# Moving the low-part subtractions of the even output projection's weights from VectorE to GpSimd

## Chip, cores and metric

One core of one Trainium2 chip runs the whole program in one launch. The metric is the device time in microseconds (us) of that core. All times below come from the runs of the kernel before, or from the trace of one profiled execution of it.

## What is computed

The reference is a two-layer decoder trunk over 256 tokens of width 1024, in float32. Cut to what matters:

```
for i in range(2):
    h = h + 0.5 * swiglu(rms_norm(h, ffa_norm[i]), ffa_w_gate_up[i], ffa_w_down[i])
    hn = rms_norm(h, mix_norm[i])
    h = h + (even_mixer(hn, ...) if i % 2 == 0 else odd_mixer(hn, ...))
    h = h + 0.5 * swiglu(rms_norm(h, ffb_norm[i]), ffb_w_gate_up[i], ffb_w_down[i])
    gate = sigmoid(rms_norm(h, ple_norm[i]) @ ple_w_gate[i])
    h = h + gate * (p[i] @ ple_w_proj[i])
return rms_norm(h, final_norm)
# even_mixer: a_q,a_k,a_v,c_q,c_kv,k_rope = split(hn @ w_in)
#   out_a = sliding-window attention with sinks (8 heads)
#   out_b = attention with low-rank q (w_uq) and kv (w_ukv), rotary part on q and k (8 heads)
#   return concatenate([out_a, out_b]) @ w_out          (1024 x 1024)
```

## The kernel before, in words

The 256 tokens are two blocks of 128 rows, t = 0 and t = 1. Each block is a Python generator (`stream`, `even`, `odd`, `ffn`, `ple`), and a loop at the end of `trunk` lets the two take turns, so that both blocks use a weight piece while it is in SBUF.

Every weight matrix is multiplied at higher precision than one pass gives: a piece is loaded as float32 into a raw tile `wr`, ScalarE (ACT) casts it to the high part `wh` (float32r), and VectorE (DVE) subtracts it from the raw piece to give the low part `wl` (`split_steps`). A product is then three matmuls: high times high, high times low, low times high. For weights without a norm gain the cast is line 240 and the subtraction line 241, both in steps of 128 x 512; with a gain they are lines 247 and 248. A list `order` holds all pieces in the order of their use; a piece is loaded four places ahead (`PREFETCH_DMA`, SP's queue, lines 221 to 226) and split one place ahead (`PREFETCH_SPLIT`). There are four raw tiles (`RAW_BUFS`) and four pairs of `wh` and `wl` (`SPLIT_BUFS`). So the load of piece i+4 waits until cast and subtraction of piece i are done, and the split of piece i+4 waits until TensorE (PE) has used piece i for both blocks.

The even output projection is `add_square("ev_out", ...)`: four pieces of 256 rows by 1024 columns, keys ("ev_out", 0) to ("ev_out", 3), no gain, each split in four steps. In `order` they stand behind the even input projection (five pieces), `uq` and `ukv`, and ahead of the second FFN's weights. Their splits therefore run while the even mixer does its attention:

- `even` makes q, k and v of both attentions: kvq scaled by ACT, the rotary part of q by DVE (lines 675, 677, 679), the rotary part of k copied into `k_f` by GpSimd (POOL) (line 753), v by DVE (line 760), then transposes by PE (line 685).
- `attend` (lines 576 to 615), for each group of heads: scores by PE (576), mask and row maximum by DVE (582), exp by ACT (588), the sink's share (594 to 596), reciprocal (598), scaling of the probabilities by DVE (600, P_sb times rinv, both in SBUF), transposes by PE (605), copy by ACT (607), product with v by PE (615).
- `mm_square` (365, 366, 369) is the output projection; line 366 is the matmul that reads `wl`.

The order of the instructions on each engine is not the program's: but for those that are pinned, a planner at build time places them by priority, by dependence and by its own estimate of each instruction's cost. Each engine then works through its list strictly in order, and waits at the head of the list for semaphores of the others. GpSimd's list in this stretch holds memsets, the two copies into `k_f` and DMAs of small tensors.

Of the kernel before, what the change touches and what calls it, by code (L numbers as in the profile page):

```python
# [10 lines left out]
F32 = mybir.dt.float32  # L11
# [30 lines left out]
def trunk(ctx, tc, a, out):  # L42
    nc = tc.nc
    pe, act, dve, pool = nc.tensor, nc.scalar, nc.vector, nc.gpsimd
# [17 lines left out]
    def pin(ins):  # L62

        return tc.keep_in_program_order(ins) if starting[0] else ins
# [76 lines left out]
    order = []  # L141
# [27 lines left out]
    for l in range(2):  # L169
        add_ffn("ffa", l)  # L170
        if l == 0:
            w = a["ev_w_in"][0]
            g = gcols["mix", 0]
            for i, k0 in enumerate((0, 3, 6)):
                kt = min(3, KD - k0)
# [50 lines left out]
            nc.sync.dma_start(r[:, :kt * n].rearrange("p (k f) -> p k f", k=kt), src)  # L226

    def split_steps(i):
        _, _, kt, n, g = order[i]
        r = raw_tiles.pop(i)  # L230
        wh = wsp.tile([P, 2048], F32R, name="wh", tag="wh")
        wl = wsp.tile([P, 2048], F32R, name="wl", tag="wl")
        tot = kt * n
        step_ = 512 if g is None else n // -(-n // 512)
        c0 = 0
        while c0 < tot:
            c1 = min(c0 + step_, tot)
            yield
            if g is None:
                pin(act.copy(wh[:, c0:c1], r[:, c0:c1]))  # L240
                pin(dve.tensor_tensor(wl[:, c0:c1], r[:, c0:c1], wh[:, c0:c1].bitcast(F32),  # L241
                                      op=ALU.subtract))
            else:
                k = c0 // n
                c1 = min(c1, (k + 1) * n)
                gc = gcol[:, g + k:g + k + 1]
                pin(act.mul(wh[:, c0:c1], r[:, c0:c1], gc))  # L247
                pin(dve.scalar_tensor_tensor(wl[:, c0:c1], r[:, c0:c1], gc,  # L248
                                             wh[:, c0:c1].bitcast(F32),
                                             op0=ALU.mult, op1=ALU.subtract))  # L250
            c0 = c1
        split_tiles[i] = (wh[:, :tot].rearrange("p (k f) -> p k f", k=kt),
                          wl[:, :tot].rearrange("p (k f) -> p k f", k=kt))
# [4 lines left out]
    def emit_split(i, steps=99):  # L258
        if i not in splits:
            splits[i] = split_steps(i)  # L260
            next(splits[i])
        for _ in range(steps):
            if next(splits[i], END) is END:
                break
# [807 lines left out]
    def at(st):  # L1072

        return index.get(st[1] if st and st[0] == "both" else st)
# [18 lines left out]
    while step != [END, END]:  # L1093
# [8 lines left out]
        else:  # L1102
            i = at(step[0]) if at(step[0]) is not None else place[0]
# [41 lines left out]
```

## Time and profile before

| | |
|---|---|
| median of 3 runs | 1045.86 us (1045.84, 1045.86, 1048.33) |
| the profiled execution | 1046.14 us, its span 1044.4 us |
| PE busy | 1026.4 us (98%) |
| DVE busy | 759.9 us (73%) |
| ACT busy | 651.1 us (62%) |
| POOL busy | 21.9 us (2%) |
| DMA, mean | 173 GB/s |

The span is what the trace covers; 1.7 us lie around it. An engine's busy time is the sum over the whole span; a change in one stretch has to be read from that stretch. In the views, "idle before" is the time for which an engine stood still ahead of an instruction, with what ended it. The chain of waits follows the work that ended last backwards through what released each step. Line numbers are those of the kernel.

### The profile page before, as it was taken

The numbers are of one execution on the slowest core, as the hardware profiler recorded it, in microseconds if no ns is written. First come the engines' busy times: TensorE is split into PE (matmuls) and PEld (weight loads), VectorE is DVE, ScalarE is ACT, GpSimd is POOL, SyncE is SP. The second block draws the span as 40 slices with busy tenths as digits, with TensorE's granted clock in tenths as the row PEclk, the third lists the DMA queues.
The fourth block names the chain that finished last, engine by engine and source line by source line (L and its number), as shares of the span: only waits on it lengthen the run. The fifth ranks groups of instructions, "written<-read, shape, count | busy, mean of one in ns | idle before, by whom it ended". The sixth has DMA issues, their size and how long they took to land.

```text
span 1044.4 us, 15663 instructions
## 1 busy us (share of the span) xinstructions
PE 1026.4 (98%) x5675; PEld 886.2 (85%) x5675; DVE 759.9 (73%) x1736; ACT 651.1 (62%) x1369; POOL 21.9 (2%) x50
## 2 busy tenths in 40 slices
PE   8999999998999999999999999999999999999996
PEld 6888888977888888888888888889998888888885
DVE  6876776888587676768868676688874868676685
ACT  6756566767576666566865656564655865656563
POOL 1000000010100000000100000001000000000000
PEclk9999999999999999999999999999999999999999
DMA  9855646453063646546565564644343465564611
GB/s 306 251 199 178 225 143 222 131 172 122 21 221 130 235 163 200 205 158 193 163 219 172 192 202 161 242 138 148 122 143 121 157 206 172 191 207 156 243 41 40
DMA packets 122189, 180.43 MB, mean 173 GB/s; under 512 B 6192, under 2 KB 96624, under 8 KB 122112
## 3 DMA queue, kind: packets, MB, share of 16 engines
q1 hardware_dynamic: 121200, 177.93, 50.8%
q0 software_dynamic: 624, 1.12, 0.3%
q8 instruction: 44, 0.72, 0.3%
q10 hardware_dynamic: 288, 0.39, 0.1%
q14 instruction: 33, 0.27, 0.1%
HBM read 178.34 MB, written 1.08 MB: 172 GB/s over the span
## 4 chain that ended last, share of the span: by engine, by line
PE 93%; DVE 3%; ACT 2%; issue 1%; DMA 1%; SPq 0%; ACTq 0%
PE tr L482 14%; PE gu L482 14%; PE acc L366 10%; PE acc L365 10%; PE acc L369 10%; PE tr L485 7%; PE gu L485 7%; PE gu L352 3%; PE gu L358 3%; PE gu L357 3%; PE acc L615 2%; PE tr L333 1%; PE tr L576 1%; PE gu L857 1%; PE gu L859 1%
## 5 line engine op out<-in xcount | busy, mean ns | idle before, releaser
L248 DVE SCALAR_TENSOR_TENSOR wl<-wr,gcol,wh 128x512 fp32r<-128x512 f32 (+2 forms) x462 | 327.4, 737 | 110.0 <-PE tr L485 88.1
L247 ACT ACTIVATE wh<-wr,gcol 128x512 fp32r<-128x512 f32 (+2 forms) x462 | 296.8, 707 | 131.6 <-PE acc L369 111.6
L482 PE MATMUL gu<-xT,wh 128*128 128x512 f32 x640 | 250.2, 391 | 0.0
L482 PE MATMUL tr<-xT,wh 128*128 128x512 f32 x640 | 249.6, 390 | 0.0
L241 DVE TENSOR_TENSOR wl<-wr,wh 128x512 fp32r<-128x512 f32 x216 | 136.2, 682 | 10.1 <-PE tr L485 5.8
L482 PEld LDWEIGHTS gu<-xT,wh 128*128 128x128 f32 x640 | 120.3, 188 | 23.6 <-ACT wh L247 0.2
L482 PEld LDWEIGHTS tr<-xT,wh 128*128 128x128 f32 x640 | 120.4, 188 | 23.6
L366 PE MATMUL acc<-wl,hT 128*128 128x512 f32 x352 | 137.6, 391 | 0.0
L365 PE MATMUL acc<-wh,hT 128*128 128x512 f32 x352 | 137.5, 391 | 0.0
L240 ACT CAST wh<-wr 128x512 fp32r<-128x512 f32 x216 | 125.3, 619 | 16.5 <-PE acc L369 11.0
L369 PE MATMUL acc<-wh,hT 128*128 128x512 f32 x352 | 109.2, 391 | 0.0
L485 PEld LDWEIGHTS gu<-xT,wl 128*128 128x128 f32 x640 | 86.8, 190 | 5.7
L485 PE MATMUL gu<-xT,wl 128*128 128x256 f32 x640 | 90.1, 283 | 0.0
L485 PE MATMUL tr<-xT,wl 128*128 128x256 f32 x640 | 89.8, 283 | 0.0
L485 PEld LDWEIGHTS tr<-xT,wl 128*128 128x128 f32 x640 | 82.5, 192 | 0.0
L369 PEld LDWEIGHTS acc<-wh,hT 128*128 128x128 f32 x352 | 66.1, 188 | 13.9
L365 PEld LDWEIGHTS acc<-wh,hT 128*128 128x128 f32 x352 | 66.3, 188 | 12.6 <-ACT hT L319 0.4
L366 PEld LDWEIGHTS acc<-wl,hT 128*128 128x128 f32 x352 | 66.3, 188 | 12.4
L490 ACT COPY sg<-gu 128x256 f32<-128x256 f32 x80 | 29.3, 366 | 74.2 <-PE gu L485 74.2
L491 DVE TENSOR_TENSOR sg<-sg,gu 128x256 f32<-128x256 f32 x80 | 33.4, 417 | 53.8 <-ACT sg L490 53.8
L319 ACT CAST hT<-sg 128x256 fp32r<-128x256 f32 x80 | 32.5, 406 | 43.0 <-DVE sg L513 43.0
L352 PE MATMUL gu<-wh,xT 128*128 128x512 f32 (+1 forms) x128 | 50.1, 392 | 0.0
(259 smaller groups left out, 1445.1 us busy)
## 6 DMA issues: line engine op xcount, KB each, us to landing
wr<-in_ffb_w_gate_up_dram SPq DMA_DIRECT2D x88, 512.0 KB, 5.3
wr<-in_ffa_w_gate_up_dram SPq DMA_DIRECT2D x84, 512.0 KB, 5.6
wr<-in_ffa_w_down_dram SPq DMA_DIRECT2D x22, 1024.0 KB, 5.0
wr<-in_ffb_w_down_dram SPq DMA_DIRECT2D x22, 1024.0 KB, 5.0
wr<-in_od_w_in_dram SPq DMA_DIRECT2D x12, 1024.0 KB, 5.1
wr<-in_ple_w_gate_dram SPq DMA_DIRECT2D x8, 1024.0 KB, 5.1
wr<-in_ev_w_out_dram SPq DMA_DIRECT2D x4, 1024.0 KB, 4.9
wr<-in_od_w_out_dram SPq DMA_DIRECT2D x4, 1024.0 KB, 5.4
```

The source lines that it names most:

```text
L240: pin(act.copy(wh[:, c0:c1], r[:, c0:c1]))
L241: pin(dve.tensor_tensor(wl[:, c0:c1], r[:, c0:c1], wh[:, c0:c1].bitcast(F32), op=ALU.subtract))
L247: pin(act.mul(wh[:, c0:c1], r[:, c0:c1], gc))
L248: pin(dve.scalar_tensor_tensor(wl[:, c0:c1], r[:, c0:c1], gc, wh[:, c0:c1].bitcast(F32), op0=ALU.mult, op1=ALU.subtract))
L319: pin(act.copy(dst_h, src))
L352: pe.matmul(dst, xh, wh, start=first, stop=False)
L365: pe.matmul(accs[n], xh, wh[:, kk, c], start=first, stop=False)
L366: pe.matmul(accs[n], xh, wl[:, kk, c], start=False, stop=False)
L369: pe.matmul(accs[n], xl, wh[:, kk, c], start=False, stop=last)
L482: pe.matmul(bv[s], w, xT[:, :, :, k, :], start=(k == 0), stop=False, skip_group_check=True)
L485: pe.matmul(bv[s][:, :, 0], w, xT[:, :, 0, k, :], start=False, stop=(k == KD - 1), skip_group_check=True)
L491: dve.tensor_tensor(o, o, bv[s][:, :, 0], op=ALU.add)
```

## The change

The subtraction of line 241 is issued on `low`, which is GpSimd for the pieces of the even output projection and VectorE for all others. Nothing else is edited.

```diff
     def split_steps(i):
-        _, _, kt, n, g = order[i]
+        key, _, kt, n, g = order[i]
+        low = pool if key[0] == "ev_out" else dve
         r = raw_tiles.pop(i)
...
             if g is None:
                 pin(act.copy(wh[:, c0:c1], r[:, c0:c1]))
-                pin(dve.tensor_tensor(wl[:, c0:c1], r[:, c0:c1], wh[:, c0:c1].bitcast(F32),
+                pin(low.tensor_tensor(wl[:, c0:c1], r[:, c0:c1], wh[:, c0:c1].bitcast(F32),
                                       op=ALU.subtract))
```

## Rows read from the trace of the kernel before

**Rows 1.** The page's chain that ended last, share of the span by engine.
```profile
PE 93%; DVE 3%; ACT 2%; issue 1%; DMA 1%; SPq 0%; ACTq 0%
```
**Rows 2.** Stretches: length, then busy us (instructions) per engine, granted clock, DMA share, GB/s.
```profile
230.00:262.00 32.00, 26.99 (x200) 23.75 (x199) 27.12 (x100) 23.40 (x82) 1.97 (x4) 1.00 0.32 100
262.00:290.00 28.00, 28.00 (x171) 24.03 (x170) 16.45 (x39) 15.17 (x36) 3.35 (x5) 1.00 0.14 42
```
**Rows 3.** PE's waits from 230 to 262 us: total us, times, longest.
```profile
PE tr L605 <- DVE rinv L598: 1.3, 1, 1.3
PE gu L685 <- DVE v_b L760: 1.2, 1, 1.2
PE acc L615 <- ACT PT_sb L607: 1.0, 2, 0.7
PE gu L352 <- ACT kT_b L687: 0.7, 1, 0.7
PE gu L605 <- DVE rsum L596: 0.6, 1, 0.6
```
**Rows 4.** Line 241 from 221 to 251.5 us: ns min/median/max, first and last start.
```profile
L241 DVE TENSOR_TENSOR wl<-wr,wh x16: 674/684/694, 221.6 to 250.4; 128x512 fp32r<-128x512 f32 x16
```
**Rows 5.** The chain of waits, 234 to 253 us: start, us, what.
```profile
236.52 0.42 DVE q_f L677
...
237.01 0.60 DVE wl L241
237.61 0.34 DVE q_f L679
...
245.37 0.16 DVE rsum L596
...
246.19 0.55 DVE P_sb L600
...
247.87 0.60 DVE P_sb L600
...
249.19 1.20 DVE wl L241 x2
...
250.47 0.60 DVE wl L241
```
**Rows 6.** ACT's instructions in order of time: start, us, what, idle before.
```profile
235.37 0.61 ACT L240 CAST wh<-wr 128x512 fp32r<-128x512 f32 x1
...
242.70 0.62 ACT L240 CAST wh<-wr 128x512 fp32r<-128x512 f32 x1
243.63 0.58 ACT L607 COPY PT_sb<-tr 128x512 f32<-128x512 f32 x1 [0.30 <-PE tr L605]
...
249.88 0.20 ACT L595 ACTIVATE sk<-sk 128x2 f32<-128x2 f32 x1
```
**Rows 7.** POOL's instructions in order of time.
```profile
210.30 0.76 POOL L753 COPY k_f<-kr 128x256 f32<-128x256 f32 x1 [205.29 <-DVE u_cq L300]
...
230.61 0.31 POOL L655 MEMSET v_c<- 128x256 f32 x1 [10.31 <-PE tr L576]
233.31 0.40 POOL L753 COPY k_f<-kr 128x256 f32<-128x256 f32 x1 [2.39 <-PE gu L685]
```
**Rows 8.** DVE's instructions around the first copy into k_f.
```profile
210.19 0.61 DVE L248 SCALAR_TENSOR_TENSOR wl<-wr,gcol,wh 128x384 fp32r<-128x384 f32 x1
210.72 0.35 DVE L302 SCALAR_TENSOR_TENSOR y_cq<-u_cq,y_cq 128x1 f32<-128x1 f32 x1
...
211.78 0.15 DVE L302 SCALAR_TENSOR_TENSOR y_cq<-u_cq,y_cq 128x1 f32<-128x1 f32 x1
```
**Rows 9.** Tile wl from 256 to 283 us, PE's matmuls that read it: ns, first and last start.
```profile
L366 PE MATMUL acc<-wl,xT x20: 387/389/398, 256.4 to 282.7; 128*128 128x512 f32 x20
```
**Rows 10.** PE's instructions in order of time: start, us, what.
```profile
239.87 0.61 PE L685 MATMUL gu<-ident,k_f 128*96 128x128 f32 x4
```
**Rows 11.** SP's queue in order of time: loads into the raw tiles that were freed.
```profile
251.13 0.37 SPq L221 DMA_DIRECT2D wr<-in_ffb_w_gate_up_dram  x1
...
284.12 0.37 SPq L226 DMA_DIRECT2D wr<-in_ffb_w_down_dram  x1
```

## Prediction before the run

> **What bounds the kernel now.** Read first the page's chain of waits: 93% of the span lies on PE and 3% on DVE [rows 1]. So work taken off DVE can shorten the kernel only where PE stands still for DVE. Next, the table of stretches, to find where that is. Around the moved work, from 230 to 262 us, PE is busy 26.99 of 32.00 us; it stands still for 5.0 us, and DVE, with 27.12 us, is the busiest engine. From 262 to 290 us PE is busy all the time [rows 2]. So this is a hole in a kernel that is otherwise bound by PE, and what it loses or gains is passed on to the end. Third, PE's own waits in that stretch: 1.3, 1.2 and 0.6 us were ended by DVE, 3.1 us in all; 1.0 and 0.7 us by ACT [rows 3]. Last, the chain of waits inside the stretch, which says what DVE did in those 3.1 us: it names the subtraction of line 241 for 0.60, 1.20 and 0.60 us, and beside it the rotation of q (L677, L679), the sum of the sinks (L596) and the scaling of the probabilities (L600) [rows 5].
>
> **What the change takes away.** Sixteen subtractions of 0.684 us leave DVE, all that start between 221.6 and 250.4 us [rows 4]: four pieces of four steps. That is 10.9 us of DVE's time, but only what lies ahead of a waiting PE counts. Three places:
> - The first subtraction in the chain (0.60 us at 237.01) lies between two steps of q's rotation, ahead of PE's wait of 1.2 us for `v_b`. Its 0.60 us are gained.
> - Ahead of PE's 0.6 us wait at L605 (for rsum), the chain runs over ACT's copy at 243.63. ACT stood idle only 0.30 us before it [rows 6], so whatever DVE does earlier, this part moves up by 0.30 us.
> - The three subtractions from 249.19 on (1.80 us on the chain) stand ahead of rinv and of the P_sb scaling at 251.18, for which PE waits 1.3 us. Not all is gained: rsum needs ACT's sk, which ends at 249.88 + 0.20 = 250.08 [rows 6]. In the chain rsum ends at 250.47, so it can move up by some 0.2 us, and the last subtraction's 0.60 us goes: 0.8 us.
>
> Gain: 0.60 + 0.30 + 0.8 = 1.7 us. Its bounds are 0 and the 3.1 us of all three waits.
>
> **What it adds on GpSimd.** No two-input operation of GpSimd is in this trace, so its length is bounded by its copy of 128 x 256, which takes 0.40 us when nothing disturbs it (at 233.31) [rows 7]. A subtraction writes 512 columns, twice as many: 0.8 us if both operands are read at once. It reads 1024, four times as many: 1.6 us if they are read in turn. I take the middle, 1.2 us, since the rows favour neither end. The sixteen make 19.2 us. [...]
>
> GpSimd's slowness by itself costs nothing, for there is room. The last cast is done at 242.70 + 0.62 = 243.3 us [rows 6]; even if four subtractions are then still to come, they end at 243.3 + 4 x 1.2 = 248.1, while PE's first matmul with these low parts starts at 256.4, and the last at 282.7 [rows 9]. Without that cover, each subtraction would cost PE up to 1.2 us. The raw tiles come free where the last subtraction ends, about when they do now, and the loads into them (the last at 251.13) are followed by none until 284.12 [rows 11]: SP's queue has tens of microseconds in hand. No DMA moves to another queue. On GpSimd's own queue stand memsets for later stages (one at 230.61) and the second copy into `k_f` at 233.31 [rows 7]; the copy is needed by PE's transposes at 239.87 [rows 10], 6.2 us after its end, room for five subtractions ahead of it. The casts stay on ACT.
>
> **What it adds on DVE.** This is the term that decides. The trace shows once what happens when GpSimd reads SBUF beside DVE. The first copy into `k_f` starts at 210.30, while DVE subtracts two SBUF operands (210.19, 0.61 us); it takes 0.76 us in place of 0.40 [rows 7, 8]. DVE's next instruction, again with SBUF operands, takes 0.35 us in place of 0.15, and both end together at 211.06 [rows 8]. So each stood still until the other had finished. [...]
>
> On the chain of this stretch five DVE instructions read two SBUF operands: L677, L679, L596 and L600 twice [rows 5]; masks and copies out of PSUM do not. The casts of the last eight steps start between 235.37 and 242.70 [rows 6], so GpSimd is busy 8 x 1.2 = 9.6 us of about 12 (236 to 248 us). A DVE instruction meets a running subtraction with a chance of 0.8, and then waits half of it, 0.6 us: 0.48 us each, five times, 2.4 us. With the ends of the price: 0.8 us gives 5 x 0.53 x 0.4 = 1.1 us; 1.6 us gives 5 x 1 x 0.8 = 4.0 us. If the two do not disturb each other, it is 0.
>
> **Sum.** -1.7 + 2.4 = +0.7 us on the profiled execution's 1046.14 us. That execution lies 0.28 us above the median of 1045.86 us, so the median after the change is 1045.86 + 0.7 = 1046.5 us (rounded down). By the two prices the sum runs from -0.6 to +2.3 us: 1045.3 to 1048.2 us. About 0.3%, or 3.1 us, is what a measurement of this kernel can tell from no change, so I forecast none.
>
> **The rivals.**
> - *GpSimd does not get in DVE's way, and all DVE waits go.* The gain is then 1.7 to 3.1 us: 1042.8 to 1044.2 us, still within 0.3%. For it: DVE is PE's releaser in three of the five lines [rows 3]. Against it: rows 7 and 8. Chance 0.13.
> - *Slower: the chain runs in step with GpSimd.* The place is 236 to 248 us, where the subtractions stand back to back; a DVE instruction that waits out one subtraction lets its successor arrive just when the next has begun. Each of the five then waits a whole one: 5 x 1.2 = 6.0 us, less 1.7: +4.3, 1050.2 us. It decides from a mean wait of (3.1 + 1.7) / 5 = 0.96 us on. For it: in the one encounter of the trace each engine waited to the other's end. Against it: the casts come from ACT with gaps, which leave GpSimd idle between subtractions. Chance 0.18.
> - *The copy into `k_f` falls behind the third piece on GpSimd's queue.* That piece's first cast ends at 235.98; four subtractions and the copy end at 235.98 + 4.8 + 0.40 = 241.2, 1.3 us after PE wants it at 239.87, or some 3 us if the casts come late. On top of the sum: 1047.8 to 1049.5 us. Against it: the copy is ready before those casts, so a planner would hardly put it last. Chance 0.07, of it 0.03 over the bound.
> - *The planner, with DVE relieved, orders all engines anew and closes the holes that ACT ends, too.* Up to 5.0 us [rows 2], less some blocking: 1041.5 us. Against it: ACT itself is busy 23.40 of 32.00 us there. Chance 0.07.
>
> That the change does not do what it says is excluded by the diff: the keys of these four pieces alone begin with "ev_out".
>
> **Numbers.** The forecast keeps 1 - 0.13 - 0.18 - 0.07 - 0.07 = 0.55. Faster by over 0.3%: the planner's 0.07. Slower by over 0.3%: 0.18 + 0.03 = 0.21. Within: 0.55 + 0.13 + 0.04 = 0.72. The range reaches down to 1042.8 us, the end of the undisturbed case, and up to 1049.7 us, into the slower case; it leaves out the planner's case and about half of the blocking one, 0.16.
>
> **What would show it.** In the changed profile, sixteen POOL instructions of line 242 with about 1.2 us each, and POOL's busy time up from 21.9 by some 19 us or more; DVE's L600, L677 and L596 between 221 and 250 us longer than before, by what they wait; PE's idle time from 230 to 262 us still near 5 us, with `v_b`, rsum and rinv or ACT behind it. Wrong would be: DVE's instructions at their old lengths beside running subtractions (then the gain stands alone); an idle time of PE of 9 us or more; PE waiting for `wl` at L366 or for `k_f` at L685; or a difference that lies outside this stretch, from an order that the planner has changed elsewhere.

## The result, and the profile after

The change makes the kernel slower. The median went from 1046.49 us (5 runs, 1045.84 to 1048.33) to 1054.11 us (5 runs, 1052.94 to 1058.95); the ratio is 1.0081, interval 1.0067 to 1.0095. No change had been forecast (1046.5 us, range 1042.8 to 1049.7 us); the median lies above that range. The profiled execution of after took 1056.97 us, 2.9 us above the median; its span is 1055.1 us.

The page first: POOL's busy time rose from 21.9 to 41.9 us, that of PE hardly (1026.4 to 1029.7 us). In the chain by engine DVE has 4% where it had 3% [rows 1].

```profile
PE 92%; DVE 4%; ACT 2%; issue 1%; DMA 1%; SPq 0%; ACTq 0%; DVEq 0%
```

The stretches (columns as in [rows 2]): from 230 to 262 us DVE is busy 25.49 us in place of 27.12, although ten of the sixteen subtractions, 6.8 us of work, left this stretch, and PE 22.34 us in place of 26.99. The granted clock, 1.00 before, is 0.84 there. It is 0.50 from 234.6 to 240 us, behind PE's long stop, and 0.57 from 254 to 258 us, behind the second one (the short stretches lie inside the long one).

```profile
230.00:234.60 4.60, 0.67 (x4) 0.39 (x3) 4.60 (x2) 1.21 (x3) 4.09 (x5) 0.90 0.83 276
234.60:240.00 5.40, 4.57 (x21) 4.04 (x22) 3.54 (x16) 1.67 (x5) 1.54 (x2) 0.50 0.00 0
254.00:258.00 4.00, 3.50 (x19) 3.53 (x20) 3.91 (x7) 1.17 (x2) 2.71 (x2) 0.57 0.55 179
230.00:262.00 32.00, 22.34 (x142) 20.11 (x142) 25.49 (x71) 19.70 (x65) 16.35 (x16) 0.84 0.44 139
262.00:290.00 28.00, 27.14 (x187) 23.77 (x188) 14.25 (x47) 12.96 (x43) 3.69 (x7) 1.00 0.01 1
```

PE's waits before were 1.3, 1.2, 1.0, 0.7 and 0.6 us [rows 3]. After (222 to 290 us; line, releaser: total us, times, longest; lines behind 229 are one higher than before), two stops stand out, both ended by DVE:

```profile
PE gu L686 <- DVE v_b L761: 5.2, 2, 4.6
PE gu L606 <- DVE P_sb L601: 2.8, 1, 2.8
PE tr L606 <- DVE P_sb L601: 1.4, 1, 1.4
```

What DVE did in those two places is in its own order of time (start, us, what). `x2` at L676 counts two instructions in 2.52 us, where 0.49 is usual; L678 and L680 take 0.42 us each undisturbed, L597 0.15 and L601 0.69:

```profile
226.25 2.52 DVE L676 TENSOR_TENSOR rot<-q_f,rope 128x128 f32<-128x128 f32 x2 [5.00 <-ACT q_f L748]
228.80 0.43 DVE L678 TENSOR_TENSOR q_f<-q_f,rope 128x256 f32<-128x256 f32 x1
229.26 5.12 DVE L680 TENSOR_TENSOR q_f<-q_f,rot 128x256 f32<-128x256 f32 x1
...
234.77 0.47 DVE L761 TENSOR_SCALAR v_b<-gu,y_ckv 128x256 f32<-128x256 f32 x1
...
250.38 0.49 DVE L583 CUSTOM_DVE_ANT_0 gu<-gu,swab,nsink 128x256 f32<-128x256 f32 x1
...
252.80 0.15 DVE L599 RECIPROCAL rinv<-rsum 128x2 f32<-128x2 f32 x1
...
253.19 1.17 DVE L601 TENSOR_TENSOR P_sb<-P_sb,rinv 128x512 f32<-128x512 f32 x1
254.28 1.22 DVE L597 TENSOR_TENSOR rsum<-rsum,sk 128x2 f32<-128x2 f32 x1
...
255.82 1.44 DVE L601 TENSOR_TENSOR P_sb<-P_sb,rinv 128x512 f32<-128x512 f32 x1
```

Beside it stands GpSimd, first as the group of line 242 (ns min/median/max, first and last start), then in order of time [rows 7]:

```profile
L242 POOL TENSOR_TENSOR wl<-wr,wh x16: 1262/1278/1713, 223.2 to 255.4; 128x512 fp32r<-128x512 f32 x16
```
```profile
226.04 2.58 POOL L242 TENSOR_TENSOR wl<-wr,wh 128x512 fp32r<-128x512 f32 x2
228.56 1.30 POOL L980 DMA_DIRECT2D p_t<-in_p_dram  x2
229.84 0.59 POOL L656 MEMSET v_b<- 128x256 f32 x2
230.37 3.72 POOL L242 TENSOR_TENSOR wl<-wr,wh 128x512 fp32r<-128x512 f32 x3
...
246.39 10.32 POOL L242 TENSOR_TENSOR wl<-wr,wh 128x512 fp32r<-128x512 f32 x8 [5.04 <-ACT wh L241]
```

Read the two lists side by side. L676's two instructions fill the time of the two subtractions that start at 226.04, one each. L680 ends at 234.38, just behind the three that end at 234.09. From 253 to 258 us, at the end of the eight subtractions that stand back to back (246.39 to 256.71), L601, L597 and L601 take 3.83 us in place of 0.69 + 0.15 + 0.69 = 1.53 us. All of these read two operands from SBUF. Two kinds keep their lengths beside the same eight subtractions: L583, one of whose operands is in PSUM (0.49 us), and the reciprocal L599, which reads one operand, from SBUF (0.15 us). The holding up goes both ways: the longest subtraction, 1.71 us, begins at 253.76, while L601 runs.

**Where the time lies.** From the first matmul of the output projection to the end of the span it is 1044.4 - 256.13 = 788.3 us before and 1055.1 - 266.82 = 788.3 us after, so all of it came ahead of that matmul. From the first `uq` matmul to it, the mixer's stretch, it is 35.4 us before and 266.8 - 222.2 = 44.6 us after: 9.2 us. (The other 1.5 us of the two profiled executions lie ahead of the stretch, in the first loads.)

### The profile page after: what moved, and what is told of

The parts are those of the page before. It is cut to its first block, busy times and chain, and to the rows that moved or that the text cites. A ratio compares the mean times of both kernels' runs of the same rounds, so it can differ in the third digit from the quotient of the medians.

```text
span 1055.1 us, 15665 instructions
## 1 busy us (share of the span) xinstructions
PE 1029.7 (98%) x5675; PEld 890.0 (84%) x5675; DVE 761.1 (72%) x1720; ACT 651.2 (62%) x1369; POOL 41.9 (4%) x66
## 4 chain that ended last, share of the span: by engine, by line
PE 92%; DVE 4%; ACT 2%; issue 1%; DMA 1%; SPq 0%; ACTq 0%; DVEq 0%
PE tr L483 14%; PE gu L483 14%; PE acc L367 10%; PE acc L366 10%; PE acc L370 10%; PE tr L486 7%; PE gu L486 7%; PE gu L353 3%; PE gu L359 3%; PE gu L358 3%; PE acc L616 2%; PE tr L334 1%; PE tr L577 1%; PE gu L858 1%; PE gu L860 1%
## 5 line engine op out<-in xcount | busy, mean ns | idle before, releaser
L366 PE MATMUL acc<-wh,hT 128*128 128x512 f32 x352 | 137.5, 391 | 0.0
L242 DVE TENSOR_TENSOR wl<-wr,wh 128x512 fp32r<-128x512 f32 x200 | 125.7, 684 | 7.9 <-PE tr L486 5.8
L366 PEld LDWEIGHTS acc<-wh,hT 128*128 128x128 f32 x352 | 66.3, 188 | 12.7 <-ACT hT L320 0.4
L353 PE MATMUL gu<-wh,xT 128*128 128x512 f32 (+1 forms) x128 | 50.1, 393 | 0.2 <-ACT wh L248 0.2
```

Of the source, the lines that this page charges most:

```text
L242: pin(low.tensor_tensor(wl[:, c0:c1], r[:, c0:c1], wh[:, c0:c1].bitcast(F32), op=ALU.subtract))
L353: pe.matmul(dst, xh, wh, start=first, stop=False)
L366: pe.matmul(accs[n], xh, wh[:, kk, c], start=first, stop=False)
```

## The experiments

The theory (P in the expectations): GpSimd's subtractions, because they read SBUF, hold up DVE's instructions that read SBUF. Rivals: the planner has put the engines into a worse order (O); GpSimd is simply late or busy. All variants but three (the last two pieces alone on GpSimd, DVE with one operand, the later subtractions on DVE) have the changed kernel's order of instructions on PE, DVE and ACT. Ratios are to the kernel before, run on the same chip. The edits are shortened: column ranges and type casts are left out, and added lines without a condition that issue on GpSimd (`pool` or `low`) hold for the four pieces of the output projection alone.

**The changed kernel again.** No edit.

> The changed kernel once more, to see what recurs from execution to execution. Theory P (port): DVE instructions with two SBUF operands stand still while GpSimd's subtractions read SBUF, PE idles behind them and its granted clock then falls. By P the long L680 (5.12 us in the first profile) or another two-operand instruction of q's rotation waits again for one or more whole subtractions of 1.28 us; total 6 to 12 us slower than before. Rival O (order): the planner's new order on PE, DVE and ACT is itself slower, and waits are the same in every execution within 0.3 us.

Measured: 1057.94 us (4 runs), 1.0099 [1.0082, 1.0116]. L680 took the same 5.12 us, PE waited 4.6 and 4.1 us, and the clock from 220 to 268 us was 0.86. The first hold-up recurs to the hundredth of a microsecond; the second varies (PE waited 2.8 us in the first profile, 4.1 us here).

**GpSimd writes, and reads nothing.** The subtraction becomes a memset of the same tile (the low parts are zero).

```diff
-pin(low.tensor_tensor(wl, r, wh, op=ALU.subtract))
+pin(pool.memset(wl, 0.0) if low is pool else dve.tensor_tensor(...))
```

> Each of the sixteen GpSimd subtractions becomes a memset of the same tile (the low parts of this weight are left out): GpSimd writes SBUF and reads nothing. The order on PE, DVE and ACT is that of the changed kernel, instruction by instruction. Theory P: no two-operand DVE instruction waits, L601 takes 0.69 us and L680 0.43; the time is between 4 us faster and 1 us slower than before. Rival O: the order is unchanged, so it stays 6 us or more slower than before.

Measured: 1046.94 us (10 runs), 1.0003 [0.9993, 1.0012]. The loss is gone with the order unchanged, so the order is not the cause. L680 is back at its length (ns min/median/max), and PE's largest wait is now one for ACT, behind it one for DVE:

```profile
L680 DVE TENSOR_TENSOR q_f<-q_f,rot x2: 424/424/425, 226.3 to 236.8; 128x256 f32<-128x256 f32 x2
```
```profile
PE gu L606 <- ACT PT_sb L608: 2.0, 1, 2.0
PE tr L606 <- DVE P_sb L601: 1.2, 1, 1.2
```

It shows a second thing: here DVE is rid of the 10.9 us and nobody holds it up, and yet the kernel is no faster than before. The expected gain of 1.7 us would be a ratio of 0.9984, outside the interval.

Because PE's order is the same in the changed kernel and in this variant, what the one loses against the other in this stretch can be divided by landmarks. PE in order of time, after:

```profile
230.28 0.38 PE L577 MATMUL tr<-kTa,qTa 128*128 128x128 f32 x2
235.29 1.09 PE L686 MATMUL gu<-ident,q_f 128*96 128x128 f32 x4 [4.63 <-DVE v_b L761]
236.18 1.92 PE L577 MATMUL tr<-kTa,qTa 128*128 128x128 f32 x8
...
240.58 0.47 PE L353 MATMUL gu<-wh,xh_cq 128*128 128x512 f32 x1
...
254.50 0.45 PE L606 MATMUL gu<-ident,P_sb 128*128 128x128 f32 x1 [2.84 <-DVE P_sb L601]
254.74 1.92 PE L616 MATMUL acc<-PT_sb,v_a 128*128 128x128 f32 x8
...
266.82 0.47 PE L366 MATMUL acc<-wh,xT 128*128 128x512 f32 x1
```

and in the write-only variant:

```profile
229.35 0.38 PE L577 MATMUL tr<-kTa,qTa 128*128 128x128 f32 x2
229.57 0.60 PE L686 MATMUL gu<-ident,q_f 128*96 128x128 f32 x4
230.00 1.06 PE L577 MATMUL tr<-kTa,qTa 128*128 128x128 f32 x8
...
232.91 0.48 PE L353 MATMUL gu<-wh,xh_cq 128*128 128x512 f32 x1
...
246.01 0.30 PE L606 MATMUL gu<-ident,P_sb 128*128 128x128 f32 x1 [2.03 <-ACT PT_sb L608]
246.15 1.06 PE L616 MATMUL acc<-PT_sb,v_a 128*128 128x128 f32 x8
...
256.87 0.47 PE L366 MATMUL acc<-wh,xT 128*128 128x512 f32 x1
```

The lag of after behind the variant is 0.93 us at L577, 5.72 at L686, 7.67 at L353, 8.49 at L606 and 9.95 at L366. By the differences, the first hold-up costs 4.79 us, the matmuls behind it 1.95 (the same eight of L577 take 1.92 in place of 1.06 us), the second hold-up 0.82 (it takes the place of a wait of 2.0 us for ACT), and what follows it 1.46, where the eight of L616 also take 1.92 us (1.06 in the variant). In all 9.02 us: 5.6 of waiting, and 3.4 that I put down mostly to the lower clock (0.50 and 0.57), which each time followed on an idle PE.

**GpSimd reads one operand.** The subtraction becomes a copy of `wh` (the low parts then hold the high ones).

```diff
+pin(pool.tensor_copy(wl, wh) if low is pool else dve.tensor_tensor(...))
```

> Each of the sixteen GpSimd subtractions becomes a GpSimd copy of the high part into the low part's tile (the product's low part is wrong by that): one SBUF operand is read in place of two. The order on PE, DVE and ACT is that of the changed kernel. Theory P, in the form that any reading by GpSimd blocks: copies of some 0.6 to 0.8 us still hold up DVE's two-operand instructions, but for half as long; 1 to 5 us slower than before. Rival form of P, that only two-operand GpSimd instructions block: as with the memsets, within 1 us of before or faster. Rival O: 6 us or more slower.

Measured: 1048.13 us (10 runs), 1.0009 [0.9998, 1.0020]. It decides nothing: a copy takes 0.62 us, half a subtraction, and hardly one of them ran beside a DVE instruction that reads two operands from SBUF. L678 at 228.50 and L680 at 228.97 kept their 0.42 us beside GpSimd's DMA issue and memsets.

**Only the last two pieces on GpSimd.**

```diff
-low = pool if key[0] == "ev_out" else dve
+low = pool if key[0] == "ev_out" and key[1] >= 2 else dve
```

> Only the last two of the four weight pieces go to GpSimd, the first two stay on DVE. Theory P: the block ahead of v_b at L680 (PE's wait of 4.6 us and the slow clock behind it) is gone, that of the probabilities' scaling (PE's waits of 2.8 and 1.4 us) stays: 1 to 5 us slower than before. Rival O: no forecast for the sum, but DVE's L601 would keep its 0.69 us.

Measured: 1050.47 us (5 runs), 1.0031 [1.0018, 1.0045]. Less than half of the loss stays, although the order is another one here. The time is where the theory put it, but not the place: the L601 kept their 0.69 us, which the expectation had named as the rival's sign. Held up were L678 at 237.92, beside the first subtraction (from 237.5 on), with 1.49 us, and L595, with 0.83 and 0.66 us in place of 0.15; PE waited 2.3 us for ACT and 1.7 us for rsum.

**Each subtraction in two halves.** The same work, in instructions of 256 columns (0.73 us). If DVE gets in at the next end of an instruction, it waits half as long.

```diff
+for b in (c0, c0 + 256): pin(low.tensor_tensor(wl[:, b:b+256], r[:, b:b+256], wh[:, b:b+256], op=ALU.subtract))
```

> Each GpSimd subtraction is cut into two of 256 columns, 32 in all; the order on PE, DVE and ACT is that of the changed kernel. What is open is for how long a waiting DVE instruction stands still. Theory P1: until the GpSimd instruction that runs is done, however many follow; then the first L680 waits at most some 0.65 us for each of two or three encounters, is under 2 us long, and the kernel is 2 to 6 us slower than before. Theory P2: until GpSimd's queue of ready instructions has run dry; then L680 stays at about 5 us, as with three whole subtractions (5.12 us), and the kernel stays 8 us or more slower.

Measured: 1052.82 us (4 runs), 1.0060 [1.0045, 1.0075]. It is 6.6 us slower than before, a little more than P1 has. Both theories meet a case: q's rotation, L676 to L680, takes turns with the halves, and none waits for more than one (P1); but L595, 0.15 us long, was passed over at several ends. In order of time, DVE and then GpSimd:

```profile
225.41 0.84 DVE L678 TENSOR_TENSOR q_f<-q_f,rope 128x256 f32<-128x256 f32 x1
226.28 0.84 DVE L680 TENSOR_TENSOR q_f<-q_f,rot 128x256 f32<-128x256 f32 x1
...
231.40 3.19 DVE L595 TENSOR_TENSOR sk<-negm,nsink 128x4 f32<-128x4 f32 x1
```
```profile
229.46 4.18 POOL L242 TENSOR_TENSOR wl<-wr,wh 128x256 fp32r<-128x256 f32 x6
233.59 0.30 POOL L656 MEMSET v_c<- 128x256 f32 x1
233.86 1.39 POOL L242 TENSOR_TENSOR wl<-wr,wh 128x256 fp32r<-128x256 f32 x2
```

L595 ended at 234.59, when the first of the last two halves did, having let the end of three or four halves and a memset go by. PE waited 3.1 us for P_sb and 2.4 us for `kT_b`.

**Two copies for each subtraction.** With the number of copies doubled, they do meet DVE.

```diff
+for _ in range(2): pin(pool.tensor_copy(wl, wh))
```

> Each GpSimd subtraction becomes two GpSimd copies of the high part (the low parts of this weight are wrong by that): GpSimd is busy as long (2 x 0.6 us in place of 1.28), but each instruction reads one SBUF operand. Order on PE, DVE and ACT as in the changed kernel. If any reading by GpSimd blocks DVE: as the half steps. If only two-operand GpSimd instructions block: DVE's L676, L678, L680, L597 and L601 keep their lengths (0.29, 0.42, 0.42, 0.16, 0.69 us) and the time is within 1.5 us of before.

Measured: 1049.57 us (5 runs), 1.0035 [1.0020, 1.0049]. L678 and L680 took 0.72 us in place of 0.42, L601 up to 1.13 us. So one operand read by GpSimd is enough to hold DVE up, here always by at most one copy; the time, 3.4 us above before, lies between the two forecasts:

```profile
225.77 0.72 DVE L678 TENSOR_TENSOR q_f<-q_f,rope 128x256 f32<-128x256 f32 x1
226.53 0.72 DVE L680 TENSOR_TENSOR q_f<-q_f,rot 128x256 f32<-128x256 f32 x1
```

**GpSimd as busy, but writing only.** Three memsets for each subtraction.

```diff
+for _ in range(3): pin(pool.memset(wl, 0.0))
```

> Each GpSimd subtraction becomes three memsets of the same tile, some 1.45 us without any read (the low parts of this weight are left out): GpSimd is busy longer than with the subtractions, its writes are three times as many. Order on PE, DVE and ACT as in the changed kernel. Theory P (reads block): DVE's instructions keep their lengths, time within 1.5 us of before. Rival: it is GpSimd's being busy or late in its queue (k_f, v_b behind it) that costs; then 4 us or more slower than before.

Measured: 1047.51 us (10 runs), 1.0010 [1.0001, 1.0020]. GpSimd was busy 26.62 of the 48 us from 220 to 268 us, in the repeated changed kernel 24.10, and L680 took 0.42 us, in the midst of memsets. Neither a busy GpSimd nor its writes are the cause of the loss of 0.8 to 1.0%; its reads of SBUF are. The 0.1% that is left wasn't followed up. This stretch, columns as in [rows 2]:

```profile
220.00:268.00 48.00, 43.28 (x297) 38.24 (x296) 30.29 (x112) 34.08 (x106) 26.62 (x57) 0.96 0.35 114
```

**DVE reads one operand.** L680 becomes a multiplication by 1.0 (the rotation's sine part is left out); GpSimd subtracts as in the change. The prediction had counted only DVE instructions with two SBUF operands; that one operand would not do was an assumption, which no run had shown.

```diff
-dve.tensor_tensor(dst, src, tmp, op=ALU.add)
+dve.tensor_scalar(dst, src, 1.0, None, op0=ALU.mult)
```

> The changed kernel, but DVE's L680 (the second half of the rotation) reads one SBUF operand in place of two: it copies by a multiplication with 1, and the rotation's sine part is left out. The first L680 stands where it stood in the order. If it is the second SBUF operand that makes DVE wait: L680 takes some 0.4 us, PE's 4.6 us wait for v_b goes, and the time is 3 to 7 us under that of the changed kernel. If DVE waits with any SBUF operand: L680 stays at several us.

Measured: 1057.73 us (2 runs), 1.0108 [1.0088, 1.0129]. The instruction, 0.29 us undisturbed, was held up as long as before. So for this kind of instruction a second operand on DVE isn't needed; for the reciprocal L599, which also reads one operand from SBUF, no hold-up is seen in any run (0.15 us in the midst of subtractions):

```profile
229.47 4.99 DVE L680 TENSOR_SCALAR q_f<-q_f 128x256 f32<-128x256 f32 x1
```

**Which half costs what.** The first two pieces subtract and the last two are memsets, then the other way round (the memset pieces have low parts of zero). The first of the two:

```diff
+pin(pool.memset(wl, 0.0) if low is pool and key[1] >= 2 else low.tensor_tensor(...))
```

> Only the first two pieces' eight subtractions read SBUF; those of the last two pieces are memsets (their low parts are left out). Order on PE, DVE and ACT as in the changed kernel. By the comparison of the changed kernel with the write-only one, step by step: PE's wait ahead of q's transposes, 4.8 us, and 1.9 us more in the matmuls that follow it at a lower granted clock; both stay here, the second hold-up (0.8 us) and its slow matmuls (1.4 us) go: some 6.5 us slower than before (5 to 8). Rival: the two hold-ups are not independent, for what is lost first is slack later; then 8 us or more.

> Only the last two pieces' eight subtractions read SBUF; those of the first two are memsets (their low parts are left out). Order on PE, DVE and ACT as in the changed kernel. By the same comparison only the second hold-up stays: 0.8 us of waiting and 1.4 us of slow matmuls, some 2 us slower than before (1 to 4). DVE's L680 takes 0.42 us both times. Rival, that the planner's order costs as well: over 5 us.

Measured: the first two alone 1054.67 us (4 runs), 1.0079 [1.0065, 1.0092]; the last two alone 1050.08 us (5 runs), 1.0034 [1.0022, 1.0046]. In the first, L680 took 5.12 us and PE waited 4.6 us for `v_b`. In the second, L680 took 0.42 us, and L597, L601 and L597 were held up:

```profile
244.10 1.30 DVE L597 TENSOR_TENSOR rsum<-rsum,sk 128x2 f32<-128x2 f32 x1
...
245.92 1.23 DVE L601 TENSOR_TENSOR P_sb<-P_sb,rinv 128x512 f32<-128x512 f32 x1
247.07 1.22 DVE L597 TENSOR_TENSOR rsum<-rsum,sk 128x2 f32<-128x2 f32 x1
```

The first two pieces make most of the loss, at the place at which the prediction hadn't looked. Their 8.6 us lie above the 5 to 8 us expected, the 4.0 us of the last two at the end of their range. The two losses, 8.6 and 4.0 us, add up to 12.6 us, more than the change's 7.6 and its repeat's 10.9 us; how they overlap wasn't resolved.

**L680 arrives a little later in GpSimd's order.** SP issues the loads of `p` in place of GpSimd, so the third run of subtractions starts ahead of L680 and not behind it. If L680's 5.12 us came from the order in which the two became ready, it should wait for one subtraction here.

```diff
-pool.dma_start(p_t, a["p"][l, 0, t * P:(t + 1) * P, :])
+nc.sync.dma_start(p_t, a["p"][l, 0, t * P:(t + 1) * P, :])
```

> The changed kernel, with the two loads of p issued by SP in place of GpSimd, so that GpSimd's third run of subtractions begins 1.3 us earlier, about where L680 becomes ready; order on PE, DVE and ACT as in the changed kernel. What is open is why the first L680 stood still through three subtractions (5.12 us), where others waited for one. Theory Q1: because it arrived while GpSimd was at a DMA and memsets with the subtractions queued behind; arriving within a subtraction it gets in behind that one: L680 under 2 us. Theory Q2: because the three subtractions had become ready in a row; it stays through all three: L680 about 3.7 us or longer.

Measured: 1050.93 us (3 runs), 1.0043 [1.0028, 1.0058]. L680 waited for the one subtraction that had begun, and got in ahead of the next; the three then take 3.92 in place of 3.72 us:

```profile
226.96 1.39 DVE L680 TENSOR_TENSOR q_f<-q_f,rot 128x256 f32<-128x256 f32 x1
228.27 0.55 DVE L321 TENSOR_TENSOR xl_cq<-tr,xh_cq 128x384 fp32r<-128x384 f32 x1
228.74 0.47 DVE L761 TENSOR_SCALAR v_b<-gu,y_ckv 128x256 f32<-128x256 f32 x1
```
```profile
226.78 3.92 POOL L242 TENSOR_TENSOR wl<-wr,wh 128x512 fp32r<-128x512 f32 x3
```

L321 and L761, which read from PSUM, run beside the second of the three at their usual lengths. PE's longest wait for `v_b` fell from 4.6 to 0.9 us; that for P_sb is 4.1 us, as in the repeat. So the length of a hold-up hangs on how the two meet. L680 did as Q1 says, and three subtractions in a row were not enough to keep it out (Q2); but L595 in the half steps arrived within a half, too, and was passed over. Why DVE is passed over in one case and not in the other stays open: in the change L680 starts at 229.26, 1.1 us before the first of the three subtractions does by the profile.

**Subtractions on DVE, but later.** An attempt to beat both: all stay on DVE, and the program issues each where the output projection first uses the piece.

> A try at a version that beats both: all sixteen subtractions stay on DVE, but are issued in the program where the output projection first uses the piece, so that the planner may place them behind the attention's own steps; it moves those of the last piece behind the P_sb scaling that the chain of the kernel before shows them ahead of. If those 1.8 us on the chain are PE's: 0.5 to 1.5 us faster than before. If ACT's copies end the wait next, as in the write-only run: within 0.5 us.

Measured: 1046.54 us (11 runs), 1.0003 [0.9994, 1.0012]. In the profile only the last piece's four subtractions moved, to behind the stretch. In place of PE's wait of 1.3 us for rinv [rows 3] there is one of 0.7 us for P_sb, and those for ACT's `PT_sb` rose from 1.0 to 1.4 us; the time stays the same, as in the write-only variant. No version was found that beats the kernel before.

## Why the prediction was wrong

**The step that failed is the cost on DVE**, the 2.4 us for "five DVE instructions", each with "a chance of 0.8" of waiting 0.6 us. The mechanism behind it holds: the write-only variants lose 0.03 and 0.10%, and the reading ones that meet DVE lose 0.3% or more. Three things were wrong with the term:

- *The place.* It counted what stands between 236 and 248 us, where the last eight casts put the subtractions. The first two pieces, whose subtractions run beside the first rotation of q from 226 to 234 us, were not looked at. They cost 6.7 us by the landmarks (4.79 + 1.95), and 8.6 us where they alone subtract. The five that it did count waited less than it said. In the profile after, the second block's L678 and L680 (244.00 and 244.46 us) and the rsum that it named (L597 at 252.52 us) kept their lengths, 0.42, 0.43 and 0.15 us; the two L601 waited some 0.5 and 0.75 us: 1.2 us together. The first place was there to be seen: the subtractions start at 221.6 [rows 4], and in the trace of before the first rotation (L675 to L679) stands in their midst, as this line of DVE's order of time shows (start, us, what):

```profile
225.73 0.42 DVE L679 TENSOR_TENSOR q_f<-q_f,rot 128x256 f32<-128x256 f32 x1
```

- *The length of one wait.* It was bounded by one subtraction (1.6 us at the most), from the single encounter in [rows 8]. L680 waited 4.7 us, through three of them.
- *The clock.* No term stood for what PE loses at the lower clock once it has stopped. [Rows 2] show a granted clock of 1.00, with no wait of PE above 1.3 us [rows 3]; after the new stops of 4.6 and 2.8 us it was 0.50 and 0.57, to which I put down most of the 3.4 us above.

The slower rival, "the chain runs in step with GpSimd" (1050.2 us, chance 0.18), came nearer, but it counted the same five instructions and bounded a wait by one subtraction, too. It named the way in which the time moved, and neither the place nor the size.

**The gain of 1.7 us did not come.** The write-only variant has the gain without the cost, and measures 1.0003. With DVE relieved, PE's largest wait there is one of 2.0 us for ACT's `PT_sb` copy, where it had been 1.3 us for DVE's rinv. That the next wait takes back just what was gained is argued from this, not shown step by step. The prediction asked at two of its three places how soon ACT ends the wait instead (its copy, 0.30 us; its sk, some 0.2 us), and took the rest as gained. The bound of 0 was named in it. With 0 the sum would have been +2.4 us, still too little.

**Right:** GpSimd's subtraction, taken as 1.2 us, measured 1.28; POOL's busy time rose by 20.0 us against "some 19". The slowness of GpSimd itself stayed covered: the last subtraction ends at 256.7, the first matmul of the output projection starts at 266.8, and PE never waited for `wl`. The second copy into `k_f` ended at 241.35 and no wait was put down to it, so that rival fell. The rival of a new order that closes ACT's holes fell, too. [Rows 8], where each engine stands still for the other, was the right row to read; the undisturbed case found no support. Of the signs named for a wrong forecast, PE's idle time "of 9 us or more" came: 32.00 - 22.34 = 9.7 us.

**The wait that the slower rival counted with.** It was one whole subtraction for each of the five instructions, taken from the one encounter in [rows 8]. In most encounters DVE waited for the rest of one instruction (L676 1.22 and 1.37 us, L597 1.22, L680 1.39 with SP's loads), in two places for several (L680 5.12 us, L595 3.19 us). The first is near what the rival had; the second, where DVE is passed over, goes beyond it.

## What to carry to other kernels

Before work that reads SBUF goes to GpSimd, list the DVE instructions on the critical path that read two operands from SBUF (here also a `tensor_scalar` with one) and stand beside it, over the whole time that GpSimd will be busy; price each with one GpSimd instruction (here most waits beside subtractions of 1.28 us were of up to 1.2 us), reckon with a whole run of them (L680 waited 4.7 us, to the end of three), and add slow matmuls where PE then stops for microseconds (here a granted clock of 0.50 and 0.57 behind stops of 4.6 and 2.8 us; but 1.00 from 220 to 268 us with the doubled copies, where PE's longest stop was 3.5 us). Work that only writes (memsets) could be put there here at a cost of some 0.1% at most (1.0003, and 1.0010 with an interval up to 1.0020). And a gain from relieving an engine counts only as far as the next engine's wait: the cheap test is a variant that drops the work altogether, in the same order.

## What the runs showed of the hardware

- DVE instructions that read two operands from SBUF were held up beside GpSimd instructions that read SBUF, with two operands (1.28 us) or one (0.62 us): L676 took 1.22 and 1.37 us in place of 0.29 beside subtractions, L678 0.72 in place of 0.42 us beside copies. A `tensor_scalar` with one operand was held up, too (4.99 in place of 0.29 us); a reciprocal with one was not (0.15 us). It could also be GpSimd that waited: with the last two pieces alone, L601 at 237.32 us kept its 0.69 us, and the subtraction that began at 237.47 took 1.67 us.
- Memsets on GpSimd left them at their lengths (L680 0.42 and L601 0.69 us beside the triple memsets), and so did DMA issue by itself (L676's two instructions 0.49 us with the single copies). Nor did subtractions hold up DVE instructions with an operand in PSUM (L583 0.49 us in the change; L321 0.55 and L761 0.47 us with SP's loads).
- A held-up DVE instruction was passed over by several GpSimd instructions in a row in two places: L680 took 5.12 us for 0.42 us of work, in all three profiles in which L680 adds and GpSimd's DMA issue stands ahead of three whole subtractions (the change, its repeat, the first two pieces), and L595 3.19 us for 0.15 us with half-sized ones. It isn't shown what decides it.
- The same eight 128 x 128 matmuls took 1.06 us at a granted clock of 1.00 and 1.92 us at 0.50, after PE had waited 4.6 us. The length of the stop isn't all that sets the clock: from 220 to 268 us it was 0.96 with the triple memsets, where PE's longest wait was 2.0 us, and 1.00 with the doubled copies, where it was 3.5 us.
